# One-column reciprocal roots on VectorE in single-tensor form, and no weight splits on GpSimd at two layer boundaries

## The chip, the cores and the metric

The kernel runs on one core of one Trainium2 chip. The metric is the device time of one launch in microseconds, as the median of several runs; the trace comes from one more execution that was recorded by the profiler. [...]

## The reference, cut to what matters

Two blocks of two layers each run on 256 rows of width 1024; the first block also carries 256 context rows through its first layer. A layer norms its rows, multiplies by wide weight matrices, mixes the rows in three branches (retention, a gated MLP and differential attention in the first block; stick-breaking, forgetting and indexed sparse attention in the second), gates and merges the branches and adds the result to the rows. The second block's layers end with an MLP of width 4096. The norms need a reciprocal root of a mean of squares per row:

```python
def _rmsnorm(x, g):
    xf = x.astype(jnp.float32)
    y = xf * lax.rsqrt(jnp.mean(xf * xf, axis=-1, keepdims=True) + NORM_EPS)
    return (y * g.astype(jnp.float32)).astype(x.dtype)
```

The layer norm inside the gated MLP needs one of the variance in the same way. All is float32.

## The kernel before, in words

**Products.** Each float32 operand is split into a high half, rounded to the format that PE multiplies fast, and a low half, the rest. `mm3` (lines 288 to 292) forms a product from three matmuls: high by high (L290), high by low (L291), low by high (L292). Weights come in units of 128 x 1024 numbers. For each unit `split_task` (lines 257 to 268) lets ACT write the high half (L265) and another engine write the low half by a subtraction (L267). That engine is DVE, except for units whose number is in the set `slow`, for which it is POOL; `slowly(k)` (line 186) puts into it the numbers that `SLOW[k]` (line 112) names, counted from the unit that comes next. `slowly(0)` is called at the second layer of the first block, `slowly(1)` and `slowly(2)` at the first and second layer of the second block, and `slowly(3)` twice, at the start of the wide MLP of each of these layers. So POOL splits units 1 to 4 at five places.

`next_unit` calls `advance` (line 273), which loads six units ahead and splits three ahead of use. The units that open a layer are therefore split while the layer before still ends.

**Layer boundaries.** At the end of a layer PE makes the last projection (`proj`, line 364 on), 128 rows at a time (a row block); its evacuation adds to the rows, takes sums of squares on ACT (L431), a reciprocal root on DVE, and transposes the rows on PE into the operand of the next layer. Where the first block passes from layer one to layer two, `update_affine` (line 540) does this for two row blocks at a time, with roots of two columns (n = 2); the scaled rows (L554) go to the transposes of L451. Where the first block passes to the second, `ev_out` (line 1243) does it per row block with n = 1: L1249 evacuates, `rms_scale` gives the root, L1257 updates the rows, `scaled_half` (line 596) transposes them (L442) and splits them (L603, L604), and `Rms.set` (line 574) takes the next root. In the second block `residual` (line 1770) does the same with L1775 and `Rms.set`, once ahead of the wide MLP and once behind it. `up` (line 1786) then evacuates its first products with L1793 and L1794 and needs that root. `end` (line 1841) closes the kernel with one root per row block.

**The root.** `rsqrt` (line 402) starts from an integer operation on the bits (L409) and refines in two steps on DVE. For n = 1 that is five SCALAR_TENSOR_TENSOR instructions with two tensors from SBUF each: L413 twice, L418, L420 and L422. `rms_scale` (line 433) puts one more of these in front (L436). There are 18 roots with n = 1: six in the layer norm (`ev_mv`, line 930) and twelve behind `rms_scale`.

**Order.** The kernel emits its work as interleaved tasks. The builder then fixes the order of each engine's instructions from its own estimate of when each is ready, so an engine's order in the trace need not be that of the source; at run time every engine works through its queue in order and waits where an operand is missing.

Of the kernel before, what the change touches and what calls it, by code (L numbers as in the profile page):

```python
# [14 lines left out]
I32 = mybir.dt.int32  # L15
AF = mybir.ActivationFunctionType
ALU = mybir.AluOpType
# [3 lines left out]
D = 1024  # L21
KT = D // P
DEPTH = 2
EPS = 1e-6
# [76 lines left out]
def two_block_kernel(ctx: ExitStack, tc: tile.TileContext, A, out):  # L101
    nc = tc.nc
    pe, dve, act, pool, sp = nc.tensor, nc.vector, nc.scalar, nc.gpsimd, nc.sync
# [5 lines left out]
    LFY = 6  # L109
    GB = 2  # L110
    GP = 2
    SLOW = [(1, 2, 3, 4), (1, 2, 3, 4), (1, 2, 3, 4), (1, 2, 3, 4)]
    cp = ctx.enter_context(tc.tile_pool(name="cp", bufs=1))
    bp = ctx.enter_context(tc.tile_pool(name="bp", bufs=25))
    kp = ctx.enter_context(tc.tile_pool(name="kp", bufs=39))
# [10 lines left out]
    def T(pool_, shape, tag, dtype=F32, bufs=None):  # L126
        kw = {} if bufs is None else {"bufs": bufs}
        return pool_.tile(shape, dtype, name=nm(tag), tag=tag, **kw)
# [78 lines left out]
    def slowly(k):  # L207
        slow.update(len(units) + i for i in SLOW[k])

    for l in range(DEPTH):  # L210
        for i, n in enumerate(ORDER1):
            w = [A["w_in"][l, n, k] for k in range(4)]
            if l == 0 and i == 0:

                m = [A["w_mod"][p, k] for p in range(4) for k in range(4)]
# [186 lines left out]
    def rsqrt(v, n, c, out=None):  # L402


        m, k = RSQRT[c]
        r = (c * 3.0 / 8.0) ** 0.2
        y = T(tp, [P, 8], "nw_y", bufs=6)[:, :n]
        t = T(tp, [P, 8], "nw_t", bufs=6)[:, :n]
        dve.tensor_scalar(y.bitcast(I32), v.bitcast(I32), -0.5, 2.0 ** 23 * (190.5 + m), op0=ALU.mult, op1=ALU.add)  # L409

        def yyv():
            if n == 1:
                dve.scalar_tensor_tensor(t, y, y, v, op0=ALU.mult, op1=ALU.mult)  # L413
            else:
                dve.tensor_tensor(t, y, y, op=ALU.mult)
                dve.tensor_tensor(t, t, v, op=ALU.mult)
        yyv()
        dve.scalar_tensor_tensor(y, t, k, y, op0=ALU.subtract, op1=ALU.mult, reverse0=True)  # L418
        yyv()
        dve.scalar_tensor_tensor(t, t, 10.0 / 3.0 * r ** 2, t, op0=ALU.subtract, op1=ALU.mult)  # L420
        o = y if out is None else out
        dve.scalar_tensor_tensor(o, t, 5.0 * r ** 4, y, op0=ALU.add, op1=ALU.mult)  # L422
        return o

    def small(n, tag="small"):
        return T(tp, [P, 8], tag, bufs=12)[:, :n]
# [6 lines left out]
    def rms_scale(sq, n=1, out=None):  # L433

        v = small(n)
        dve.scalar_tensor_tensor(v, sq[:, 0:n], D * EPS, sq[:, n:2 * n], op0=ALU.add, op1=ALU.add)  # L436
        return rsqrt(v, n, D ** 0.5, out)

    def transposed4(src):
# [99 lines left out]
    def update_affine(x, osb, sqo, hT, s, mods):  # L539

        rs = rms_scale(sqo, 2)
        sq = small(4)
        for i in range(2):
            for c in range(2):
                dve.scalar_tensor_tensor(x[i][c], osb[i][c], rs[:, i:i + 1], x[i][c], op0=ALU.mult, op1=ALU.add)
            sum_sq(x[i], sq, i, 2)
            yield
        rs = rms_scale(sq, 2)
        yield
        xn = [[None, None] for _ in range(2)]  # L550
        for c in range(2):
            for i in range(2):
                xn[i][c] = t2([P, 512])
                dve.tensor_scalar(xn[i][c], x[i][c], rs[:, i:i + 1], None, op0=ALU.mult)  # L554
            yield
        for p in range(0, 4, 2):
            ps = [transposed_quarter(xn, p + k) for k in range(2)]
            yield
            g = [affine(hT, s, p + k, ps[k], mods, k == 1, pool if s else dve) for k in range(2)]
            for _ in range(3):  # L560
                for x in g:
                    next(x, None)
                yield

    class Rms:
# [9 lines left out]
        def set(self, x, tb):  # L575
            sq = small(2)
            sum_sq(x, sq)
            rms_scale(sq, 1, self(tb))
            dve.tensor_scalar(self(tb, True), self(tb), 0.5, None, op0=ALU.mult)
# [275 lines left out]
    def block1_layer(l, hT, xin, t_norm):  # L855
# [76 lines left out]
        def ev_mv(tb, ps):  # L932
            v = vn[tb] = copy_tile(ps)
            st = T(tp, [P, 6], "bnst", bufs=4)
            dve.bn_stats(st, v)
            mv = small(2)
            dve.bn_aggr(mv, st)
            var = small(1)
            dve.tensor_scalar(var, mv[:, 1:2], EPS, None, op0=ALU.add)
            rs = rsqrt(var, 1, 1.0)  # L940
            dve.tensor_scalar(v, v, mv[:, 0:1], rs, op0=ALU.subtract, op1=ALU.mult)
# [117 lines left out]
        def ret_task(tb):  # L1059
# [34 lines left out]
            v = small(4)  # L1094
            dve.tensor_scalar(v, sq, P * EPS, None, op0=ALU.add)
            rs = rsqrt(v, 4, P ** 0.5)
            o = o1
            for h in range(4):
# [835 lines left out]
```

## Time and profile before

| | |
|---|---|
| median of 3 runs | 1860.49 us (1858.41 to 1860.88) |
| the profiled execution's own time | 1861.23 us |
| its span, first to last instruction | 1859.4 us |
| mean granted TensorE clock | 0.994 |
| busy: PE, DVE, ACT, POOL | 98%, 66%, 48%, 11% |
| weight splits on POOL (L267) | 21 of 2.4 us |
| weight splits on DVE (L267) | 437 of 1.3 us |

The profile is of one execution. In a row of the timeline the first number is the start of an instruction in microseconds from the start of the span, the second its length. Then stand the engine, the line of the source, the operation, what it writes and reads, and how many such instructions stand in the row. A bracket at the end of a row gives the idle time of the engine just before it and whose work ended that idle time. The profile counts an instruction as busy from its start on its engine, so time in which it is held up after it has started is part of its length.

### The profile page before, as it was taken

To read this page: it belongs to the slowest core of one execution; us is meant where nothing else is said; L and a number is where in the kernel's file an instruction comes from. 1 tells how busy PE (TensorE), PEld (TensorE's weight loads), DVE (VectorE), ACT (ScalarE), POOL (GpSimd) and SP (SyncE) were. 2 spreads that over 40 slices of the span, in tenths; PEclk is the share of its full clock that TensorE was granted. 3 is DMA by queue.
4 is the path that set the end of the run, shared out by engine and by line. 5 is a ranking of instruction groups with operands and counts; after the bars stand their busy time and mean duration, and the time that the engine had idled before them with its cause. 6 is when DMAs were issued, how large, how long until landed. Compare 5 with 4: busy or idle time off the path is not lost.

```text
span 1859.4 us, 25881 instructions
## 1 busy us (share of the span) xinstructions
PE 1813.5 (98%) x9704; PEld 1516.0 (82%) x9704; DVE 1218.9 (66%) x2414; ACT 888.1 (48%) x1557; POOL 200.0 (11%) x135
## 2 busy tenths in 40 slices
PE   8999999999999999999999999999999999999998
PEld 4888888887888878878888777789978877778997
DVE  4755546567775844578789886555567978665555
ACT  4624233445343433465464675444446468444443
POOL 2020000001101110001020023100011003320000
PEclk9999999999999999999999999999999999999999
DMA  9533223323462332445744355445554435544552
GB/s 322 181 121 124 92 71 128 104 95 114 147 215 92 130 102 72 147 144 194 264 139 140 125 171 165 160 152 191 185 178 147 129 122 181 170 159 162 189 188 96
DMA packets 83613, 279.34 MB, mean 150 GB/s; under 512 B 13856, under 2 KB 14240, under 8 KB 83360
## 3 DMA queue, kind: packets, MB, share of 16 engines
q1 hardware_dynamic: 83488, 277.70, 44.8%
q8 instruction: 76, 1.25, 0.3%
q14 instruction: 49, 0.40, 0.1%
HBM read 276.61 MB, written 1.05 MB: 149 GB/s over the span
## 4 chain that ended last, share of the span: by engine, by line
PE 40%; DVE 8%; ACT 2%; POOL 2%; issue 1%; DMA 0%; DVEq 0%; POOLq 0%; ACTq 0%
PE mm L290 9%; PE mm L291 9%; PE mm L292 9%; PE sm L290 3%; PE sm L292 3%; PE sm L291 3%; DVE k L267 2%; POOL k L1734 1%; PE sm L442 1%; PE sm L1432 1%; PE sm L1421 1%; ACT k L265 1%; POOL k L1732 1%; DVE k L1604 1%; DVE nw_t L413 1%
## 5 line engine op out<-in xcount | busy, mean ns | idle before, releaser
L290 PE MATMUL mm<-k,k 128*128 128x512 f32 (+1 forms) x2192 | 834.9, 381 | 2.4 <-ACT k L466 2.4
L292 PE MATMUL mm<-k,k 128*128 128x512 f32 (+1 forms) x2192 | 822.9, 376 | 1.1 <-DVE k L267 0.8
L291 PE MATMUL mm<-k,k 128*128 128x512 f32 (+1 forms) x2192 | 823.8, 376 | 0.0
L267 DVE TENSOR_TENSOR k<-k,k 128x1024 fp32r<-128x1024 f32 x437 | 547.4, 1269 | 185.0 <-ACT k L265 123.0
L265 ACT ACTIVATE k<-k 128x1024 fp32r<-128x1024 f32 x458 | 475.1, 1056 | 329.2 <-DVE k L267 142.9
L290 PEld LDWEIGHTS mm<-k,k 128*128 128x128 f32 x2192 | 413.8, 189 | 78.0 <-issue 6.0
L292 PEld LDWEIGHTS mm<-k,k 128*128 128x128 f32 x2192 | 413.8, 189 | 76.7 <-DVE k L468 1.3
L291 PEld LDWEIGHTS mm<-k,k 128*128 128x128 f32 x2192 | 414.6, 189 | 67.2 <-issue 0.5
L290 PE MATMUL sm<-k,k 128*128 128x256 f32 (+1 forms) x504 | 149.1, 296 | 0.0
L291 PE MATMUL sm<-k,k 128*128 128x256 f32 (+1 forms) x504 | 146.2, 290 | 0.0
L292 PE MATMUL sm<-k,k 128*128 128x256 f32 (+1 forms) x504 | 146.2, 290 | 0.0
L1803 DVE SCALAR_TENSOR_TENSOR k<-sm,k 128x512 f32<-128x512 f32 x28 | 19.4, 692 | 123.4 <-PE sm L292 123.4
L290 PEld LDWEIGHTS sm<-k,k 128*128 128x128 f32 x504 | 96.8, 192 | 3.8 <-issue 2.8
L267 POOL TENSOR_TENSOR k<-k,k 128x1024 fp32r<-128x1024 f32 x21 | 50.4, 2416 | 455.7 <-ACT k L265 214.3
L292 PEld LDWEIGHTS sm<-k,k 128*128 128x128 f32 x504 | 96.5, 192 | 1.7 <-issue 0.7
L291 PEld LDWEIGHTS sm<-k,k 128*128 128x128 f32 x504 | 96.6, 192 | 1.3
L1805 ACT ACTIVATE k<-k 128x512 f32<-128x512 f32 x28 | 17.4, 622 | 140.0 <-DVE k L1803 140.0
L652 DVE CUSTOM_DVE_ANT_0 k<-k,k 128x1024 f32<-128x1024 f32 x56 | 68.8, 1233 | 23.4 <-PE mm L291 20.3
L913 POOL TENSOR_TENSOR k<-k,k 128x512 f32<-128x512 f32 x16 | 23.4, 1467 | 289.9 <-DVE k L911 289.0
L298 DVE TENSOR_TENSOR k<-sm,k 128x256 fp32r<-128x256 f32 (+2 forms) x78 | 31.8, 413 | 31.4 <-ACT k L297 30.6
L442 PE MATMUL sm<-cst,k 128*128 128x128 f32 x232 | 37.5, 287 | 15.2 <-DVE k L1775 6.9
L442 PEld LDWEIGHTS sm<-cst,k 128*128 128x128 f32 x232 | 28.3, 146 | 27.6 <-DVE k L1775 10.1
(288 smaller groups left out, 1631.2 us busy)
## 6 DMA issues: line engine op xcount, KB each, us to landing
k<-in_w_in SPq DMA_DIRECT2D x248, 512.0 KB, 3.5
k<-in_w_up SPq DMA_DIRECT2D x64, 512.0 KB, 3.6
k<-in_w_down SPq DMA_DIRECT2D x64, 512.0 KB, 3.5
k<-in_w_bo SPq DMA_DIRECT2D x48, 512.0 KB, 3.5
k<-in_w_modT SPq DMA_DIRECT2D x32, 512.0 KB, 3.5
k<-in_w_out SPq DMA_DIRECT2D x32, 512.0 KB, 3.7
k<-in_w_mod SPq DMA_DIRECT2D x16, 512.0 KB, 7.8
k<-in_c_rows SPq DMA_DIRECT2D x5, 512.0 KB, 3.8
```

Of the source, the lines that this page charges most:

```text
L265: act.activation(h, r, AF.Copy)
L267: (pool if i in slow else eng).tensor_tensor(lo, r, h.bitcast(F32), op=ALU.subtract)
L290: pe.matmul(ps, lh, rh, start=start, stop=False)
L291: pe.matmul(ps, lh, rl, start=False, stop=False)
L292: pe.matmul(ps, ll, rh, start=False, stop=stop)
L298: dve.tensor_tensor(lo, src, h.bitcast(F32), op=ALU.subtract)
L413: dve.scalar_tensor_tensor(t, y, y, v, op0=ALU.mult, op1=ALU.mult)
L442: pe.transpose(ps[:, k], src[:, k * P:(k + 1) * P], ident)
L652: dve.tensor_tensor_reduce(o, w, sb[s], 0.5, 0.0, op0=ALU.mult, op1=ALU.add, accum_out=res[:, s, i - 1:i])
L913: pool.tensor_tensor(o, o, tt, op=ALU.add)
L1421: pe.transpose(pt[:, j, sb * P:(sb + 1) * P], z[:, j, sb * P:(sb + 1) * P], ident)
L1803: dve.scalar_tensor_tensor(r, ps, 0.0, rms_h.row()[:, None, :].to_broadcast([P, 2, 256]), op0=ALU.max, op1=ALU.mult)
```

## The change

It has two parts. `SLOW` loses its first two entries, so the eight units that POOL split at the last boundary inside the first block and at the boundary between the blocks are split by DVE; the other two entries stay. And the root for n = 1 takes TENSOR_SCALAR: one tensor from SBUF and up to two scalars per partition, which are the other columns. TENSOR_SCALAR has no reversed operand order, so the first guess gets the opposite sign (the -256 in the constant flips the sign bit) and the first refinement turns it back. Roots of more columns keep their form.

```diff
-    SLOW = [(1, 2, 3, 4), (1, 2, 3, 4), (1, 2, 3, 4), (1, 2, 3, 4)]
+    SLOW = [(), (), (1, 2, 3, 4), (1, 2, 3, 4)]
...
-        dve.tensor_scalar(y.bitcast(I32), v.bitcast(I32), -0.5, 2.0 ** 23 * (190.5 + m), op0=ALU.mult, op1=ALU.add)
+        o = y if out is None else out
+        one = n == 1
+
+        dve.tensor_scalar(y.bitcast(I32), v.bitcast(I32), -0.5, 2.0 ** 23 * (190.5 + m - 256.0 * one),
+                          op0=ALU.mult, op1=ALU.add)
+
+        def times(dst, a, x, b, op):
+
+            if one:
+                dve.tensor_scalar(dst, a, x, b, op0=op, op1=ALU.mult)
+            else:
+                dve.scalar_tensor_tensor(dst, a, x, b, op0=op, op1=ALU.mult, reverse0=(dst is y and op == ALU.subtract))
 
         def yyv():
-            if n == 1:
-                dve.scalar_tensor_tensor(t, y, y, v, op0=ALU.mult, op1=ALU.mult)
+            if one:
+                times(t, y, y, v, ALU.mult)
             else:
                 dve.tensor_tensor(t, y, y, op=ALU.mult)
                 dve.tensor_tensor(t, t, v, op=ALU.mult)
         yyv()
-        dve.scalar_tensor_tensor(y, t, k, y, op0=ALU.subtract, op1=ALU.mult, reverse0=True)
+        times(y, t, k, y, ALU.subtract)
         yyv()
-        dve.scalar_tensor_tensor(t, t, 10.0 / 3.0 * r ** 2, t, op0=ALU.subtract, op1=ALU.mult)
-        o = y if out is None else out
-        dve.scalar_tensor_tensor(o, t, 5.0 * r ** 4, y, op0=ALU.add, op1=ALU.mult)
+        times(t, t, 10.0 / 3.0 * r ** 2, t, ALU.subtract)
+        times(o, t, 5.0 * r ** 4, y, ALU.add)
         return o
...
-        dve.scalar_tensor_tensor(v, sq[:, 0:n], D * EPS, sq[:, n:2 * n], op0=ALU.add, op1=ALU.add)
+        if n == 1:
+            dve.tensor_scalar(v, sq[:, 0:1], D * EPS, sq[:, 1:2], op0=ALU.add, op1=ALU.add)
+        else:
+            dve.scalar_tensor_tensor(v, sq[:, 0:n], D * EPS, sq[:, n:2 * n], op0=ALU.add, op1=ALU.add)
```

## Rows read from the trace of the kernel before

**Rows 1.** The page, busy time of each engine with its share of the span.
```profile
PE 1813.5 (98%) x9704; PEld 1516.0 (82%) x9704; DVE 1218.9 (66%) x2414; ACT 888.1 (48%) x1557; POOL 200.0 (11%) x135
```

**Rows 2.** Timeline of PE around the boundaries: start, length, work, idle time before it.
```profile
594.43 0.39 PE L290 MATMUL mm<-k,k 128*128 128x512 f32 x1
...
599.87 0.28 PE L290 MATMUL mm<-k,k 128*128 128x256 f32 x1
...
609.33 0.66 PE L451 MATMUL sm<-cst,k 128*128 128x128 f32 x2 [4.58 <-DVE k L554]
...
939.96 1.09 PE L442 MATMUL sm<-cst,k 128*128 128x128 f32 x4 [3.12 <-DVE k L1257]
...
1208.97 0.66 PE L442 MATMUL sm<-cst,k 128*128 128x128 f32 x4 [1.20 <-DVE k L1775]
...
1218.83 0.66 PE L442 MATMUL sm<-cst,k 128*128 128x128 f32 x4 [1.25 <-DVE k L1794]
...
1395.60 1.12 PE L442 MATMUL sm<-cst,k 128*128 128x128 f32 x4 [4.51 <-DVE k L1775]
```

**Rows 3.** PE by stretch: stretch, its length, PE busy (x instructions), granted clock, DMA.
```profile
1395.60:1400.76 5.16, 5.16 (x16) 0.50 0.47 164
1199.00:1218.80 19.80, 17.38 (x82) 1.00 0.56 183
```

**Rows 4.** Timeline of POOL at the same places.
```profile
591.63 7.11 POOL L267 TENSOR_TENSOR k<-k,k 128x1024 fp32r<-128x1024 f32 x3 [46.31 <-ACT k L265]
...
930.54 4.77 POOL L267 TENSOR_TENSOR k<-k,k 128x1024 fp32r<-128x1024 f32 x2 [10.03 <-ACT k L265]
...
1206.30 4.74 POOL L267 TENSOR_TENSOR k<-k,k 128x1024 fp32r<-128x1024 f32 x2 [1.97 <-ACT k L265]
...
1386.52 7.07 POOL L267 TENSOR_TENSOR k<-k,k 128x1024 fp32r<-128x1024 f32 x3 [175.49 <-DVE k L1775]
```

**Rows 5.** Timeline of DVE, first block, from layer one to two.
```profile
592.77 1.29 DVE L436 SCALAR_TENSOR_TENSOR small<-sqs 128x2 f32<-128x2 f32 x1
594.09 2.33 DVE L409 TENSOR_SCALAR nw_y<-small 128x2 int32<-128x2 int32 x1
596.46 2.30 DVE L415 TENSOR_TENSOR nw_t<-nw_y 128x2 f32<-128x2 f32 x1
```

**Rows 6.** Timeline of DVE, from the first block to the second.
```profile
930.60 2.36 DVE L422 SCALAR_TENSOR_TENSOR rms<-nw_t,nw_y 128x1 f32<-128x1 f32 x1
932.99 0.15 DVE L579 TENSOR_SCALAR rms<-rms 128x1 f32<-128x1 f32 x1
...
935.66 2.39 DVE L413 SCALAR_TENSOR_TENSOR nw_t<-nw_y,small 128x1 f32<-128x1 f32 x1
```

**Rows 7.** Timeline of DVE, second block, from layer one to two.
```profile
1387.34 1.59 DVE L436 SCALAR_TENSOR_TENSOR small<-small 128x1 f32<-128x1 f32 x1 [0.26 <-ACT k L431]
1388.97 0.15 DVE L409 TENSOR_SCALAR nw_y<-small 128x1 int32<-128x1 int32 x1
...
1389.56 1.75 DVE L413 SCALAR_TENSOR_TENSOR nw_t<-nw_y,small 128x1 f32<-128x1 f32 x1
1391.34 2.26 DVE L418 SCALAR_TENSOR_TENSOR nw_y<-nw_t,nw_y 128x1 f32<-128x1 f32 x1
```

**Rows 8.** Timeline of DVE ahead of the wide MLP of the second block's layer one.
```profile
1202.08 2.27 DVE L413 SCALAR_TENSOR_TENSOR nw_t<-nw_y,small 128x1 f32<-128x1 f32 x1
...
1206.51 0.61 DVE L604 SCALAR_TENSOR_TENSOR k<-sm,g,k 128x128 fp32r<-128x128 f32 x2 [0.85 <-ACT k L603]
...
1208.24 0.68 DVE L1775 TENSOR_TENSOR k<-mm,k 128x512 f32<-128x512 f32 x1
```

**Rows 9.** DVE prices: a line's instructions with least, median and greatest ns; one timeline row.
```profile
L413 DVE SCALAR_TENSOR_TENSOR nw_t<-nw_y,small x36: 206/219/2393, 56.5 to 1854.3; 128x1 f32<-128x1 f32 x36
...
L420 DVE SCALAR_TENSOR_TENSOR nw_t<-nw_t x36: 142/159/1275, 9.5 to 1854.6; 128x1 f32<-128x1 f32 x18, 128x4 f32<-128x4 f32 x12, 128x2 f32<-128x2 f32 x6
...
602.63 1.22 DVE L267 TENSOR_TENSOR k<-k,k 128x1024 fp32r<-128x1024 f32 x1
```

## The prediction, made before the changed kernel was built or run

> **What bounds the kernel now.** I read the busy table first: PE is busy 98% of the span [rows 1], so a change on DVE or POOL can only give back what PE still idles, or the time that its clock is low. I therefore went next to PE's timeline and looked for brackets. The large ones stand at boundaries [rows 2]: 4.58 us ahead of L451, waiting for L554; 3.12 us ahead of L442, for L1257; 1.20 and 1.25 us ahead of the wide MLP, for L1775 and L1794 (the other layer of the second block shows the same pair, 1.20 and 1.35); and 4.51 us, again for L1775. Call the places, in order of time, A (609), B (940), C (1209 to 1219, and its twin C' at 1670), and D (1396). Each wait is for DVE, at the end of a chain of norm work.
>
> The third view is PE's clock. [...]
>
> Fourth, DVE's timeline ahead of each wait, beside POOL's. One-column instructions that last 0.16 or 0.22 us in the middle of their group [rows 9] last 1.6 to 2.4 us there [rows 5 to 8], and each long one ends when a POOL split ends. At D, POOL's three splits run from 1386.52, 2.36 us each [rows 4], so they end at 1388.88, 1391.24 and 1393.59; the long L436, L413 and L418 end at 1388.93, 1391.31 and 1393.60 [rows 7]. So a DVE instruction with two tensors from SBUF is held up until POOL's instruction is over, and that falls into the chain that PE waits for.
>
> Which forms are held decides this change. L409 with one column, between the held L436 and L413, took 0.15 us [rows 7], although POOL's second split was on; with two columns at place A the same line took 2.33 [rows 5]. L579, one column and one tensor, took 0.15 within POOL's second split at B [rows 4, 6]. L604 reads one tensor from PSUM, one from SBUF and a scalar per partition, and took 0.61 for two within POOL's split at C [rows 4, 8]. So a form with one SBUF tensor of one column escapes, and a scalar per partition does not make it wait.
>
> [...]
>
> **The change, part by part.** I sum against the profiled execution's own time, 1861.23 us, which is 0.74 above the median of the runs.
>
> The price of the new form: L413 has one scalar per partition more than L420 and lasts 219 against 159 ns [rows 9], so a scalar costs about 60 ns. Every changed instruction turns one tensor into such a scalar: six per root behind an `rms_scale`, 0.35 us; 18 roots, some 6 us of DVE in all. It matters only where a root stands on a chain that PE waits for: three roots at B, one at C, C' and D each, one at the end of the kernel. The six of the layer norm lie beside products on PE that show no such wait. No row shows a one-column TENSOR_SCALAR with two scalars; bounds are nothing (one tensor less) and twice the price; I take 60 ns by the nearest rows.
>
> Place A (roots of two columns, so only `SLOW` acts). Three POOL splits held L436, L409 and L415 for 1.13 + 2.17 + 2.14 = 5.44 us over 0.16 each [rows 5]. They go. The three splits come to DVE, 1.22 us each [rows 9], and DVE was busy without a gap there, so 3.66 come back on the same chain. Gain 1.8. The fourth split, at 542, lies far ahead, where DVE has slack until the layer ends. If the splits found gaps, the wait could go wholly, 4.6; if DVE's order were worse, nothing. The wait that stays, 2.8, is nearer to the 3.1 of B than to the 1.2 of C, so I let the clock fall as before.
>
> Place B. Held: L422 for 2.20 and L413 for 2.17 [rows 6], 4.37 in all. Added: three splits, 3.66 (the fourth, at 918, ran while DVE idled), and three dearer roots, 1.05. Net 0.3 lost. Bounds: the whole wait of 3.1 gained; 1.6 lost with the fourth split on the chain too.
>
> Place D (POOL still splits). L436, L413 and L418 lose 1.43 + 1.53 + 2.10 = 5.06 [rows 7], against 0.35 for the form. Then L1775 no longer waits for DVE but for its products, which end at 1395.60 - 4.51 = 1391.09. What is late next is L1775 itself, 0.68 us [rows 8] and some 0.2 for the two handovers: a wait of 0.9 stays, 3.6 go. [...] Gain 6.2; bounds 0 and 7.1.
>
> Places C and C' (POOL still splits). L413 loses 2.05 [rows 8], less 0.35: all behind it moves up by 1.7, L1775 from 1208.24 to 1206.5, and ends at 1207.2, before PE's 1207.77 (1208.97 - 1.20). The first wait goes if the products that L1775 reads are done by then. PE then comes 1.2 earlier to the second wait, whose chain moves up by 1.7 less one more dear root, 1.3: PE gains 1.3, and 1.1 of that wait stays. Twice 1.3 is 2.6; bounds 0 and 5.0, all four waits.
>
> The end of the kernel: nothing covers the last root, 0.35 lost.
>
> Sum: 1.8 - 0.3 + 6.2 + 2.6 - 0.35 = 9.95. 1861.23 - 9.95 = 1851.3 for such an execution, less 0.74 for the median: **1850.5 us**. No DMA is added or moved to another queue; POOL loses 8 splits of 2.4 us and nobody else waits for it there.
>
> **Rivals.**
> 1. The moved splits eat more. DVE is the engine that ends the waits at A and B, and its order is made anew. With nothing gained at A, C and C', the sum is 6.2 - 0.3 - 0.35 = 5.5, so 1855.0 (1851.6 to 1856.3 by the bounds of B, 1857.6 if the clock also falls at D). For: DVE has no gap at A. Against: 5.44 of holding is more than 3.66 of splits.
> 2. The change does not do what it says: the new form is held too. Then only A gains: 1.8 - 0.3, less 0.35 at D, at C, at C' and at the end, 0.1 in all, so 1860.4. For: no row shows exactly this form. Against: L409, L579 and L604.
> 3. Slower: low halves come too late for PE. PE begins to read the first moved split at 594.43 and the third at 599.87 [rows 2], 2.72 us per unit of twelve products; POOL's three end at 594.0, 596.4 and 598.7 [rows 4], just ahead. If DVE takes them only behind L554, the products between 594.43 and 604.75 (609.33 - 4.58), 10.3 us, no longer cover the chain, and at B, with six products per unit, two units or 2.7. Then 13.0 lost against 6.2 + 2.6 - 0.35 gained is 4.6 slower, 1865.0. It decides once the two places lose over 12.2, which is all of this cover but 0.8. Against: the splits' high halves are ready early, and the order takes what is ready.
>
> **How the numbers follow.** About 0.2%, 3.7 us, is what a measurement of this kernel can tell from no change; that is 1856.8 and 1864.2. My forecast has 0.58, rival 1 0.25 (a quarter of it within 0.2%), rival 2 0.12 and rival 3 0.05. Faster: 0.58 + 0.19 = 0.77; the same: 0.06 + 0.12 = 0.18; slower: 0.05. The range takes in the forecast with the open bounds of A and C on the gain's side, 2.8 + 2.4 = 5.2 more, so 1845 in round numbers, and rival 1 to its end, 1858; it leaves out rivals 2 and 3.
>
> **What would show it.** Right: no DVE instruction of one column over 0.4 us under a POOL split; L436, L413 and L418 at 0.2 to 0.3 us each as TENSOR_SCALAR; at D a wait of under 1.3 and the clock at 1.00; C and C' with about 1.1 of waiting in place of 2.5; no POOL split near 592 or 931, and three DVE splits more there, with waits of about 2.8 and 3.4. Wrong: new roots that still last 1.6 to 2.4 (rival 2), a wait at L291 or L292 for DVE L267 at 594 to 600 or 934 (rival 3), or waits at A and B as long as before (rival 1). If PE's order differs so that the waits stand elsewhere, the sum by place fails even where the total holds.

## The result, and the profile after

The changed kernel takes **1845.95 us** (median of 4 runs, 1843.43 to 1846.06) against 1860.68 of the kernel before on the same chip: ratio 0.9918 [0.9901, 0.9935]. A second set gave 1846.02 against 1861.42, ratio 0.9919 [0.9906, 0.9933]. So it is faster by 15 us where 10 were forecast; the range held it, by 0.95 us at its lower end. The sum by place shows that this is not the forecast with a size off: one place paid three and a half times what I had put down, and one lost more than I had put down.

Code lines below the root are numbered 13 higher in the changed kernel: L554 is L567, L1257 is L1270, L451 is L464, L442 is L455, L1249 is L1262, L1775 is L1788, L1794 is L1807, L604 is L617, L579 is L592. L436 became L447 (L449 for two columns), L409 is L412, and L413, L418, L420 and L422 are L418 for one column.

The busy table after, which answers to [rows 1], shows PE as the bound still (PE is TensorE, DVE VectorE, ACT ScalarE, POOL GpSimd):

```profile
PE 1809.0 (98%) x9704; PEld 1511.6 (82%) x9704; DVE 1208.3 (66%) x2422; ACT 887.3 (48%) x1557; POOL 182.1 (10%) x127
```

To place the gain I took seven waits of PE that both kernels have and compared the stretches between them. First the timeline of PE before (start, length, work, idle time ahead and what ended it); the wait at 1218.83 that belongs to the list stands in [rows 2], and the row at 603.90 is a short wait within A that is needed below:

```profile
584.64 0.44 PE L451 MATMUL sm<-cst,k 128*128 128x128 f32 x2 [0.64 <-DVE k L554]
...
603.90 0.39 PE L292 MATMUL mm<-k,k 128*128 128x256 f32 x1 [0.76 <-DVE k L267]
...
695.37 0.66 PE L442 MATMUL sm<-cst,k 128*128 128x128 f32 x4 [0.56 <-POOL k L913]
...
813.90 0.63 PE L1180 MATMUL sm<-cst,k 128*128 128x128 f32 x4 [0.43 <-DVE k L1176]
...
989.30 0.60 PE L1566 MATMUL sm<-cst,lf 128*40 128x256 f32 x2 [0.77 <-issue]
...
1450.80 0.60 PE L1566 MATMUL sm<-cst,lf 128*40 128x256 f32 x2 [0.72 <-DVE lf L1560]
...
1678.57 0.66 PE L442 MATMUL sm<-cst,k 128*128 128x128 f32 x4 [1.35 <-DVE k L1794]
```

And the timeline of PE after, with the waits at A (610.02) and B (935.43) among them:

```profile
584.77 0.44 PE L464 MATMUL sm<-cst,k 128*128 128x128 f32 x2 [0.65 <-DVE k L567]
...
610.02 0.41 PE L464 MATMUL sm<-cst,k 128*128 128x128 f32 x2 [0.54 <-DVE k L567]
...
688.98 0.66 PE L455 MATMUL sm<-cst,k 128*128 128x128 f32 x4 [0.50 <-POOL k L926]
...
807.51 0.63 PE L1193 MATMUL sm<-cst,k 128*128 128x128 f32 x4 [0.44 <-DVE k L1189]
...
935.43 1.86 PE L455 MATMUL sm<-cst,k 128*128 128x128 f32 x8 [3.75 <-DVE k L1270]
...
984.14 0.60 PE L1579 MATMUL sm<-cst,lf 128*40 128x256 f32 x2 [0.76 <-issue]
...
1211.79 0.66 PE L455 MATMUL sm<-cst,k 128*128 128x128 f32 x4 [0.71 <-DVE k L1807]
...
1436.74 0.60 PE L1579 MATMUL sm<-cst,lf 128*40 128x256 f32 x2 [0.82 <-DVE lf L1573]
...
1662.65 0.66 PE L455 MATMUL sm<-cst,k 128*128 128x128 f32 x4 [0.84 <-DVE rms L592]
```

| place, between the waits | before, us | after, us | gained | forecast |
|---|---|---|---|---|
| A, 584.64 to 695.37 | 110.73 | 104.21 | 6.5 | 1.8 |
| B, 813.90 to 989.30 | 175.40 | 176.63 | -1.2 | -0.3 |
| C, 989.30 to 1218.83 | 229.53 | 227.65 | 1.9 | 1.3 |
| D, 1218.83 to 1450.80 | 231.97 | 224.95 | 7.0 | 6.2 |
| C', 1450.80 to 1678.57 | 227.77 | 225.91 | 1.9 | 1.3 |
| from there to the end of the span | 180.83 | 181.25 | -0.4 | -0.35 |

These six give 15.7, and the start loses 0.13 (584.64 to 584.77): 15.6, beside 15.5 between the two spans, which are printed to a tenth (1859.4 and 1843.9). The stretch between A and B, 118.53 us in both, shows how well a stretch repeats where nothing changes and the clock stays up (1.00 in both). Where the clock falls, as at B (0.58 from 939.96 to 944.00 before, 0.51 from 935.43 to 938.93 after), a stretch repeats less well. There, three traces with the changed kernel's order of PE (this one, that of the second set, and that of `early_a` below) took 176.63, 175.99 and 175.47, and four with the order of before (that of before and the three late runs below) took 174.62 to 175.59. So the loss at B is some 0.9 us, and the 1.2 of one pair of traces is not sure to better than 1 us.

**The new form escapes.** The timeline of DVE at D, and one of POOL there, answer to [rows 7] and [rows 4]:

```profile
1380.30 0.21 DVE L447 TENSOR_SCALAR small<-small 128x1 f32<-128x1 f32 x1 [0.26 <-ACT k L441]
...
1381.14 0.26 DVE L418 TENSOR_SCALAR nw_t<-nw_y,small 128x1 f32<-128x1 f32 x1
...
1383.18 0.69 DVE L1788 TENSOR_TENSOR k<-mm,k 128x512 f32<-128x512 f32 x1 [0.33 <-PE mm L292]
```

```profile
1379.48 9.50 POOL L267 TENSOR_TENSOR k<-k,k 128x1024 fp32r<-128x1024 f32 x4 [175.59 <-DVE k L1788]
```

POOL splits from 1379.48 to 1388.98, and the root within it runs at its unhindered price. L1788 now waits for its products on PE (its bracket names L292), and the transposes behind it show no wait. The clock stays up behind these transposes, where it was 0.50 before [rows 3]. The view of stretches (stretch, its length, PE, PEld, DVE, ACT, POOL, granted clock, DMA share, GB/s):

```profile
1383.90:1388.00 4.10, 4.10 (x23) 3.44 (x23) 2.82 (x11) 3.88 (x11) 4.10 (x3) 1.00 0.72 237
```

The view of one line, with least, median and greatest length in ns, shows that the root is held nowhere in the run; its first row answers to L413 in [rows 9], where the greatest was 2393:

```profile
L418 DVE TENSOR_SCALAR nw_t<-nw_y,small x36: 237/269/276, 56.6 to 1838.5; 128x1 f32<-128x1 f32 x36
L418 DVE TENSOR_SCALAR nw_y<-nw_t,nw_y x28: 201/212/219, 56.9 to 1839.1; 128x1 f32<-128x1 f32 x28
```

The one-column form is not held: 276 ns at most, where the two-column L409 took 2.33 us under such a split [rows 5].

**A, though, was not won there.** Its roots have two columns and kept their form. L567 does not even start earlier than L554 did (609.38 after, 608.71 before): six splits, not three, stand on DVE between 590 and 600. DVE's timeline before, and then after:

```profile
608.71 1.67 DVE L554 TENSOR_SCALAR k<-k,nw_y 128x512 f32<-128x512 f32 x4
```

```profile
591.70 1.23 DVE L267 TENSOR_TENSOR k<-k,k 128x1024 fp32r<-128x1024 f32 x1
...
593.44 2.35 DVE L267 TENSOR_TENSOR k<-k,k 128x1024 fp32r<-128x1024 f32 x2
...
596.21 1.23 DVE L267 TENSOR_TENSOR k<-k,k 128x1024 fp32r<-128x1024 f32 x1
...
597.82 1.23 DVE L267 TENSOR_TENSOR k<-k,k 128x1024 fp32r<-128x1024 f32 x1
...
599.46 1.23 DVE L267 TENSOR_TENSOR k<-k,k 128x1024 fp32r<-128x1024 f32 x1
...
609.38 1.68 DVE L567 TENSOR_SCALAR k<-k,nw_y 128x512 f32<-128x512 f32 x4
```

What changed is PE's queue. The builder has put the transposes of L464 47 places later (numbers 2687 to 2703 by the count that the expectations below use, 2640 to 2656 before; among the matmuls of the trace the 2975th to 2991st, and the 2928th to 2944th before), so PE has products until 609.48 (610.02 - 0.54) and waits 0.54 us instead of 4.58. By the view of stretches, the clock stays at 1.00 through A. Before:

```profile
609.00:613.00 4.00, 3.67 (x20) 3.70 (x21) 3.49 (x7) 1.47 (x4) 0.00 (x0) 0.59 0.00 0
```

After, A and then B, where it still falls, to 0.51:

```profile
609.00:613.00 4.00, 3.46 (x31) 3.25 (x30) 3.93 (x9) 2.74 (x5) 0.00 (x0) 1.00 0.77 267
...
935.43:938.93 3.50, 3.50 (x13) 3.08 (x14) 2.28 (x10) 3.07 (x10) 0.00 (x0) 0.51 0.44 144
```

The 6.5 of A are thus 4.0 of waiting (4.58 - 0.54), up to 1.6 of clock (0.41 of the 4.00 us in the row of before, of which 0.33 were still waiting) and the 0.76 us wait for a split (L267) which stood in the kernel before at 603.90 and is gone.

### The profile page after: what moved, and what is told of

Read it like the earlier page. It is cut to its first block, busy times and chain, and to the rows that moved or that the text cites. A ratio compares the mean times of both kernels' runs of the same rounds, so it can differ in the third digit from the quotient of the medians.

```text
span 1843.9 us, 25880 instructions
## 1 busy us (share of the span) xinstructions
PE 1809.0 (98%) x9704; PEld 1511.6 (82%) x9704; DVE 1208.3 (66%) x2422; ACT 887.3 (48%) x1557; POOL 182.1 (10%) x127
## 5 line engine op out<-in xcount | busy, mean ns | idle before, releaser
L292 PE MATMUL mm<-k,k 128*128 128x512 f32 (+1 forms) x2192 | 821.1, 375 | 0.3 <-DVE k L481 0.3
L267 DVE TENSOR_TENSOR k<-k,k 128x1024 fp32r<-128x1024 f32 x445 | 555.7, 1266 | 184.3 <-ACT k L265 121.0
L292 PEld LDWEIGHTS mm<-k,k 128*128 128x128 f32 x2192 | 412.9, 188 | 75.4 <-DVE k L481 1.4
L292 PE MATMUL sm<-k,k 128*128 128x256 f32 (+1 forms) x504 | 146.2, 290 | 0.0
L292 PEld LDWEIGHTS sm<-k,k 128*128 128x128 f32 x504 | 96.5, 192 | 1.6 <-issue 0.7
L1818 ACT ACTIVATE k<-k 128x512 f32<-128x512 f32 x28 | 17.4, 623 | 140.0 <-DVE k L1816 140.0
L267 POOL TENSOR_TENSOR k<-k,k 128x1024 fp32r<-128x1024 f32 x13 | 31.0, 2403 | 284.7 <-DVE k L1788 175.6
L297 ACT ACTIVATE k<-sm 128x256 fp32r<-128x256 f32 (+2 forms) x78 | 28.7, 374 | 46.0 <-PE sm L455 18.0
L441 ACT ACTIVATE k<-k 128x512 f32<-128x512 f32 x36 | 22.6, 628 | 52.7 <-DVE k L1788 22.1
```

Of the source, the lines that this page charges most:

```text
L267: (pool if i in slow else eng).tensor_tensor(lo, r, h.bitcast(F32), op=ALU.subtract)
L292: pe.matmul(ps, ll, rh, start=False, stop=stop)
L297: act.activation(h, src, AF.Copy)
L441: act.activation(t2([P, 512]), x[c], AF.Square, accum_out=sq[:, c * n + i:c * n + i + 1])
```

## The experiments

Where a run is compared by place, the stretches are those of the table.

### 1. One half of the change at a time

`slow_only` is the kernel before with the changed `SLOW`:

```diff
-    SLOW = [(1, 2, 3, 4), (1, 2, 3, 4), (1, 2, 3, 4), (1, 2, 3, 4)]
+    SLOW = [(), (), (1, 2, 3, 4), (1, 2, 3, 4)]
```

> The old one-column root, and POOL splits nothing at places A and B, as in the change. Theory (the new form pays at C, C' and D, the moved splits pay at A): the long L436, L413 and L418 and the waits of 4.5 us at D and of 1.2 and 1.25 at C and C' are back; A is as in the changed kernel (PE waits about 0.5, clock stays up), 6.4 gained; B is about 0.5 slower than before. About 1854.5 us. Rival (all of the gain is the new form's): 1860, with a wait of over 4 us at A.

Measured: 1851.0 us, ratio 0.9950 [0.9935, 0.9965].

`form_only` is the changed kernel with the `SLOW` of before, so the diff's other half alone.

> The new one-column root, and POOL splits four units at each of the five places, as before. Theory: D gains 7.0, C and C' 1.85 each, the end loses 0.4, all as in the changed kernel; A is as before (PE waits 4.6, the clock falls), since its roots have two columns; at B the roots are no longer held under POOL's splits, which gains up to 3. About 1847.5 us. Rival (POOL's splits hold other DVE work at B, so nothing is gained there): 1850.5.

Measured: 1850.17 us, ratio 0.9945 [0.9930, 0.9960].

| | before | slow_only | form_only | after |
|---|---|---|---|---|
| A, us | 110.73 | 104.23 | 112.02 | 104.21 |
| B, us | 175.40 | 172.03 | 172.60 | 176.63 |
| C, us | 229.53 | 229.51 | 227.68 | 227.65 |
| D, us | 231.97 | 231.17 | 225.04 | 224.95 |

C and D belong to the form and A to the moved splits: PE's order of work is the same before and in `form_only` everywhere but near B, so C and D do not gain by another order of PE. The 1.3 us that `form_only` loses at A are the clock's: the wait there is as before (4.57), but from 609 to 617 the granted clock was 0.57, where it was 0.80 before.

Both runs missed what I expected. `slow_only` missed by 3.5 us because B gained 3.4 where I had put a loss. `form_only` missed by 2.7; its time is that of the rival (1850.5), but B did gain the 2.8 that the rival denied, and what is lacking are the 1.3 at A and another 1.3 ahead of A (its first wait comes at 585.93, before at 584.64). At B, then, each half gains by itself (3.4 and 2.8) and the two together lose. Some of the 2.8 is the clock's too: `keep_b` below has the same order of PE's work there, its clock fell to 0.77 where that of `form_only` was 1.00, and it gains 1.3. PE's timelines at B, for `slow_only`, then for `form_only`:

```profile
932.72 1.29 PE L442 MATMUL sm<-cst,k 128*128 128x128 f32 x8 [0.86 <-DVE k L1257]
```

```profile
941.10 0.63 PE L455 MATMUL sm<-cst,k 128*128 128x128 f32 x4 [1.53 <-DVE k L1270]
```

Before the wait is 3.12 [rows 2], and with both halves 3.75.

### 2. Is A's gain the place in PE's queue?

`early_a` is the changed kernel, in which products at A may no longer be put ahead of the transposes (a dependency of order alone, without a semaphore):

```diff
+                        mark = len(nc.cur_bb.bb.instructions)
...
+                        if u * (4 // m) + q >= behind:
+                            for i in nc.cur_bb.bb.instructions[mark:]:
+                                for t in anchor:
+                                    if i.engine == t.engine:
+                                        tc.add_manual_dep(i, t.name, mybir.DependencyInfo(
+                                            mybir.DependencyClass.NoSync, mybir.DependencyReason.DATA), reason="behind")
...
+            if s:
+                anchor.append(nc.cur_bb.bb.instructions[-1])
...
-        projT(4, mov, ev_mg, n=n, ticks=1)
+        projT(4, mov, ev_mg, n=n, ticks=1, behind=3 if last else 99)
```

> The changed kernel, but PE's transposes at place A (L464 there) are put back in PE's queue to where they stood before, some 40 products of 0.12 us earlier, by an order dependency alone. Theory (the gain at A came from PE's queue, in which the builder put the transposes 47 products later once DVE had the splits; DVE's chain is not earlier): PE waits 4 to 5 us at A again and its clock falls, 5 to 6 us slower than the changed kernel, 1851.5 us. Rival (the gain at A came from DVE no longer being held, the order is only its result): under 1 us slower, 1846 to 1847.

Measured: 1851.81 us, ratio 0.9952 [0.9937, 0.9967]; A takes 109.69. The wait is back at its old length, although POOL splits nothing near it, and the clock falls behind it (PE's timeline, then the view of stretches, of `early_a`):

```profile
608.37 3.38 PE L471 MATMUL sm<-cst,k 128*128 128x128 f32 x16 [4.51 <-DVE k L576]
```

```profile
608.37:611.75 3.38, 3.38 (x18) 3.23 (x19) 2.03 (x5) 1.28 (x3) 0.00 (x0) 0.58 0.00 0
```

PE's order differs from that of the changed kernel in these places alone (59 of 9704 matmuls, the 2933rd to the 2991st); DVE's order behind them, from 607 to 630, was made anew with it. So the late place is necessary. Whether it is enough, the next runs ask of the kernel before, where POOL still splits at A. `late_a10` delays the second half's transposes by ten ticks (a tick is one turn of the interleaved tasks):

```diff
+        yield from wait(10 if s else 0)
         for p in range(0, 4, 2):
             ps = [transposed_quarter(xn, p + k) for k in range(2)]
```

> This is the kernel before (old root, POOL splits at the same places) with one thing added: at A the second half's transposes are issued ten ticks later by their task, which puts them 53 places later in PE's queue (number 2693 instead of 2640; the changed kernel has them at 2687). POOL still subtracts there, so VectorE's two-column root is still held. Theory (A's gain came from the place of the transposes in PE's queue alone): the 4.58 us wait of PE at A falls under 1.5 us, the clock no longer falls there, and the time is the kernel before's less 5 to 6.5 us, about 1854.5. Rival (A's gain needs VectorE free of POOL's hold): the root still ends as late as before, PE waits as long, only later, and the time stays within 1.5 us of the kernel before's, 1859 to 1861.

Measured: 1859.54 us, ratio 0.9991 [0.9981, 1.0000]. The time is the rival's (1859 to 1861), but its reason is not quite what happened: the wait at A is gone, and a new one of 3.02 us stands at 634.94, behind other work of DVE (L958). It could have come from the second batch of transposes, which came out 49 places behind the first in the order of PE. `late_four9` and `late_four10` issue all sixteen together, after nine and ten ticks:

```diff
+        if s:
+            yield from wait(9)
+            four = [transposed_quarter(xn, k) for k in range(4)]
         for p in range(0, 4, 2):
-            ps = [transposed_quarter(xn, p + k) for k in range(2)]
+            ps = four[p:p + 2] if s else [transposed_quarter(xn, p + k) for k in range(2)]
```

> Kernel before, POOL splitting as there, with all sixteen transposes of the second half at A issued together, 41 places later in PE's queue (2681 to 2696; before 2640 to 2656, the changed kernel 2687 to 2703). The last run put them in two batches 49 places apart and removed the 4.58 us wait at A, but a new one of 3.02 us, with the clock down for twice as long, came at 635, behind VectorE's L958, 26 us later. Theory (place in PE's queue alone sets A; the second batch's lateness made the new wait): A's wait under 1 us, no fall of the clock there, no new wait over 1 us until 690, time 1854 to 1856. Rival (in the kernel before the VectorE work behind A is late as well, so that moving the transposes only shifts the wait): a wait of 2 us or more between 612 and 640, time 1858 to 1861.

> The same with the sixteen transposes 53 places later (2693 to 2708). Theory: no wait at A at all, no new wait over 1 us until 690, time 1853.5 to 1856. Rival: a wait of 2 us or more between 612 and 640, time 1858 to 1861.

Measured: 1858.42 us, ratio 0.9986 [0.9977, 0.9996], and 1862.41 us, ratio 1.0004 [0.9994, 1.0013]. The rival holds, though the second run lies 1.4 us above its range: the place alone only shifts the wait. In `late_four9` PE goes through the transposes at 609.76 without any wait, as good as after the change, and then stands at 633 for DVE's L960 (L957 before, L970 after); PE's timeline of `late_four9`, and then of `late_four10`:

```profile
633.29 0.47 PE L290 MATMUL mm<-k,k 128*128 128x512 f32 x1 [2.62 <-DVE k L960]
```

```profile
636.02 0.77 PE L290 MATMUL mm<-k,k 128*128 128x512 f32 x1 [3.98 <-DVE k L960]
```

DVE's timelines say what differs. That evacuation starts at 632.39 before, 632.47 in `late_four9`, and 625.08 after:

```profile
632.39 1.28 DVE L957 TENSOR_TENSOR k<-mm,k 128x512 f32<-128x512 f32 x2
```

```profile
632.47 0.68 DVE L960 TENSOR_TENSOR k<-mm,k 128x512 f32<-128x512 f32 x1
```

```profile
625.08 0.69 DVE L970 TENSOR_TENSOR k<-mm,k 128x512 f32<-128x512 f32 x1
```

In the kernel before this was hidden, because PE lost its time at A already. After the change DVE is not held between 592 and 599: by 600 us, 95 low halves have been written (94 on DVE, 1 on POOL) against 93 (88 and 5), and the work behind A comes 7 us sooner. These late runs also move DVE's own order: its evacuations of the transposes (L464) start at 618.21 in `late_four9` and at 610.89 before. A version that moves PE's transposes and leaves DVE's order as it was has not been tried, so how the 7 us divide between the missing hold and the builder's new order on DVE stays open. `early_a` narrows it, for POOL holds nothing at A there either. Its evacuation, in DVE's timeline:

```profile
630.27 0.68 DVE L981 TENSOR_TENSOR k<-mm,k 128x512 f32<-128x512 f32 x1
```

Counted from the wait that opens the table's first stretch (584.17 in `early_a`), it starts only 1.7 us sooner than before. PE's wait at A is the same in both, so the two compare: with PE's transposes early, the missing hold does not bring the 7 us by itself.

### 3. What B wants

`keep_b` is the changed kernel with POOL's splits back at B alone:

```diff
-    SLOW = [(), (), (1, 2, 3, 4), (1, 2, 3, 4)]
+    SLOW = [(), (1, 2, 3, 4), (1, 2, 3, 4), (1, 2, 3, 4)]
```

> The changed kernel, but POOL splits its four units at place B again. Theory (the splits that went to DVE at B cost more than POOL's, now that the roots are not held): B gains about 4.5 against the changed kernel, by less waiting for L1270 and a clock that stays up; 1841.5 us. Rival (POOL's splits hold L1270 or DVE's own splits in place of the roots): 1845 to 1847.

Measured: 1843.16 us, ratio 0.9908 [0.9891, 0.9924], between theory and rival; B takes 174.13, and the wait there is 1.50. Against the three traces with the changed kernel's order at B that is 1.3 to 2.5 us less. So with the new root POOL's splits at B are better kept, but the gain is small beside the spread of B, and the intervals of the two ratios, from two sets of runs, overlap.

`old_b` goes the other way: no splits of POOL at B, and the old root in the first block:

```diff
-        one = n == 1
+        one = n == 1 and state["block"] == 2
...
+    state["block"] = 2
     for l in range(DEPTH):
         h_acts, rms2 = block2_layer(l, h_acts, rms2)
```

> This is the changed kernel with the old two-tensor root in the first block alone, up to and with B; from the second block on, where POOL still subtracts, it has the new form, and POOL subtracts nothing at A and B as in the change. PE's queue has the same order as in the run with the moved subtractions alone, where B cost 4.6 us less than in the changed kernel (172.03 us from the wait at about 807 to the next shared event at about 980, against 176.63). Theory (what the change loses at B is the new form's longer root with more of the low halves put between its steps, and the old root is free where POOL is silent): PE's wait at B is under 1.5 us instead of 3.75 and the clock does not fall there, C, C' and D stay gone, 1841.4 us, faster than both kernels and than the run in which POOL keeps its subtractions at B (1843.16). Rival (the loss at B is the moved subtractions themselves, whatever the root): B's wait stays above 3 us and the time at 1845 to 1847.

Measured: 1840.02 us, ratio 0.9890 [0.9876, 0.9905]; B takes 171.44, the wait is 0.86, and the clock stays at 1.00 (931.40 to 934.90). DVE's timelines show where the time went. After the change, the last root of B, with two splits among its steps:

```profile
930.84 0.27 DVE L418 TENSOR_SCALAR nw_t<-nw_y,small 128x1 f32<-128x1 f32 x1
931.15 0.21 DVE L418 TENSOR_SCALAR nw_y<-nw_t,nw_y 128x1 f32<-128x1 f32 x1
931.28 1.22 DVE L267 TENSOR_TENSOR k<-k,k 128x1024 fp32r<-128x1024 f32 x1
932.41 0.27 DVE L418 TENSOR_SCALAR nw_t<-nw_y,small 128x1 f32<-128x1 f32 x1
932.72 0.21 DVE L418 TENSOR_SCALAR nw_t<-nw_t 128x1 f32<-128x1 f32 x1
933.14 1.23 DVE L267 TENSOR_TENSOR k<-k,k 128x1024 fp32r<-128x1024 f32 x1 [0.21 <-issue]
934.29 0.21 DVE L418 TENSOR_SCALAR nw_y<-nw_t,nw_y 128x1 f32<-128x1 f32 x1
934.53 1.41 DVE L1270 SCALAR_TENSOR_TENSOR k<-k,nw_y,k 128x512 f32<-128x512 f32 x2
```

The same root in the old form, in `slow_only` (`old_b` has the same order on PE, and its root runs from 929.42 to L1270 at 930.51 with the next split at 931.84):

```profile
930.74 0.22 DVE L413 SCALAR_TENSOR_TENSOR nw_t<-nw_y,small 128x1 f32<-128x1 f32 x1
...
931.63 0.16 DVE L422 SCALAR_TENSOR_TENSOR nw_y<-nw_t,nw_y 128x1 f32<-128x1 f32 x1
931.83 1.41 DVE L1257 SCALAR_TENSOR_TENSOR k<-k,nw_y,k 128x512 f32<-128x512 f32 x2
933.16 1.22 DVE L267 TENSOR_TENSOR k<-k,k 128x1024 fp32r<-128x1024 f32 x1
```

From its first L413 to L1257 are 1.1 us; from the first L418 to L1270, 3.7. The new form makes up some 0.3 of the difference, five steps at 0.05. The other 2.3 are the two splits, which the builder has put between the steps of the longer root; in the other kernel no split stands there, and the next one comes behind L1257. PE's order is no rival for this: it differs at B between the changed kernel and `old_b` (43 matmuls), but the transposes that wait are the 4593rd to 4600th matmul in both. To make sure, the changed kernel and `old_b` ran once more side by side.

> The changed kernel once more, on the same chip and beside the same runs of the kernel before as the next one. It was 1845.95 us, ratio 0.9918 [0.9901, 0.9935]. Theory and rival both expect 1844 to 1847 here, ratio 0.990 to 0.994.

> The changed kernel with the old root in the first block alone, once more, now beside the changed kernel itself. It was 1840.02 us, ratio 0.9890 [0.9876, 0.9905], in another set of runs. Theory (it gains the 4.6 us of B): 1839 to 1842, its interval below the changed kernel's. Rival (the difference came from the set of runs): within 2 us of the changed kernel, intervals overlapping for the most part.

Measured: 1846.02 (1845.27 to 1847.08), ratio 0.9919 [0.9906, 0.9933], and 1841.85 (1841.03 to 1842.75), ratio 0.9895 [0.9881, 0.9908]. No run of one reaches the other. The mixed version, the old root up to B and the new one in the second block, is 4.2 us faster than the change and beats both kernels.

## Why the prediction was right, and where it was not

**The form** was right: which instructions are held, that one column with scalars escapes, and the price, 269 against 219 ns with one scalar more (50 where I had 60). Rival 2 falls with it: none of the L418 lasts over 276 ns.

**D** was right in its mechanism: 7.0 where I had 6.2. I had left 0.9 us of waiting behind L1775; no wait stands there, and the clock is 1.00 behind it (1383.90 to 1388.00), so the term all but reached its bound of 7.1. Of the 6.2, 2.6 were the clock's, half of the 5.16 us at 0.50 [rows 3]; that it would stay up behind a wait of 0.9 was my estimate from the 1.20 at C with the clock at 1.00 [rows 3], and with no wait at D it was not put to the test there. In the five traces that have the old root there D took 230.98 to 232.27, and in the seven with the new root 224.93 to 225.04, so the gain is 5.9 to 7.3.

**C and C'** were right: 1.9 each for 1.3. The first wait is gone as forecast, and 0.71 and 0.84 stay of the second, where I had 1.1.

**A failed**, by the step "3.66 come back on the same chain. Gain 1.8", and by the one after it, "The wait that stays, 2.8". Six splits came to that chain, it ends 0.67 us later than before, and still the wait fell to 0.54. I had held PE's queue fixed and asked when DVE would be done, although the front of this document says that the builder makes the order anew. What the runs show in its place has two halves, and neither is enough: the transposes stand 47 places later in PE's queue (undone in `early_a`, 5.9 us in all and 5.5 at A), and DVE's work behind A comes 7 us sooner (without it, the late runs gain at most 2.4 us). The line on the whole wait, "4.6", came nearer, but A went beyond it by 1.9, because it left out the clock, which I had let fall, and the wait at 603.90. The prediction's last sentence had said that the sum by place fails if PE's order differs; that is what happened, but no term had been put on it.

**B** lost 1.2 in this pair of traces, some 0.9 over all, for 0.3, within its bound of 1.6; the wait is 3.75 where I had about 3.4. Rival 1 had this mechanism, moved splits that eat more, and it holds at B alone: five splits stand on DVE's chain from 925 on (I counted three), two of them inside the last root. What I did not see is that the two halves of the change spoil each other here. With the old root three splits stand ahead of L1257, the number that I had counted, and B gains 3.4; with POOL's splits kept the new root gains 1.3 or 2.8.

**Rival 3** did not happen: no product of PE waits for a low half around A or B.

That the total came within the range is partly luck. A gained more than the bound that I had given it, and the range held only because it also kept 2.4 us open for C and C', of which 1.2 were used, and because B lost more. By the stretches of the two traces the single sum was 5.6 us off (15.6 for 9.95): A alone is 4.7 of it, D, C and C' add 2.0, and B and the start take back 1.1. By the medians it was 4.6 off.

## What to carry to other kernels

When an edit changes which engine does a piece of work, and a builder orders the queues from estimates, look at the order of the built queues beside the durations: here 47 places in PE's queue, with DVE's work behind them 7 us sooner, were worth 6.5 us, and the places alone at most 2.4. Try the halves of a change apart and by place; the new root was right at C and D, and at B only as long as POOL kept its splits there, and the mix is better than the change. And a wait that goes may only have hidden the next one: see when the consumer behind it would have been ready.

## What the runs showed of the hardware that was not expected

- The clock behind a wait of 1.5 us went both ways. At B, `keep_b` (wait 1.50) and `form_only` (wait 1.53) have the same work behind it. The view of stretches, of `keep_b`, then of `form_only`:

```profile
932.11:935.61 3.50, 2.93 (x13) 2.32 (x14) 3.41 (x6) 3.50 (x9) 1.97 (x3) 0.77 0.01 2
```

```profile
941.10:944.60 3.50, 2.93 (x16) 2.35 (x17) 3.41 (x6) 3.50 (x9) 1.97 (x3) 1.00 0.01 2
```

  The stretch B is 1.5 us longer where it fell. In `late_four9` it stayed at 1.00 behind 2.62 us (633.29 to 636.70), and in `late_four10` it was 0.50 behind 3.98. What decides between is not settled here.
- An instruction on large tensors is held under POOL's splits too: in `keep_b` the two L1270 at B took 2.73 us, beside 1.41 after the change, where POOL is silent. The timelines of POOL and of DVE in `keep_b`:

```profile
924.30 7.12 POOL L267 TENSOR_TENSOR k<-k,k 128x1024 fp32r<-128x1024 f32 x3 [11.06 <-ACT k L265]
```

```profile
929.90 2.73 DVE L1270 SCALAR_TENSOR_TENSOR k<-k,nw_y,k 128x512 f32<-128x512 f32 x2
```

  So POOL's splits at B are not free with the new root either; they are the lesser loss.
